# A second plain pair in the second feed-forward network, and a plain down step cut in two around the last unit

## The chip, the cores and the metric

One NeuronCore of a Trainium2 chip runs the whole block. TensorE (PE) does the matrix products, VectorE (DVE) and ScalarE (ACT) the elementwise work; SyncE (SP) issues plain DMA transfers and GpSimd (POOL) those that also convert or accumulate. The metric is the device time of one execution in microseconds.

## The reference

A decoder block on 512 tokens of width 1024, in float32. The change concerns its two gated feed-forward networks (hidden width 2816) and the first product behind the first of them.

```python
def swiglu(x, w_gate, w_up, w_down):
    return (jax.nn.silu(x @ w_gate) * (x @ w_up)) @ w_down

h = h + 0.5 * swiglu(rms_norm(h, g_ffn1[i]), w_ffn1_gate[i], w_ffn1_up[i], w_ffn1_down[i])
u = rms_norm(h, g_mix[i])
z = u @ w_in[i]
...
h = h + (g_a * y_conv + g_b * y_attn) @ w_mix_out[i]
h = h + 0.5 * swiglu(rms_norm(h, g_ffn2[i]), w_ffn2_gate[i], w_ffn2_up[i], w_ffn2_down[i])
```

## The kernel before

**Numbers.** Every float32 operand is used as a high and a low part, and a product is three matmuls (high x high, high x low, low x high). Weights get their parts in one of two ways. Either SP loads them into `wr`, ACT copies the high part (`wh`) and DVE subtracts (`wl`), in `split_one`. Or ACT writes the negated copy to `wl` and a POOL transfer adds the weights on top (`remainder`, L369 and L371); for keys in `by_dma` that are not products, POOL also loads `wh`. The gate and up weights of the second network's plain pairs are of this last kind, those of the first network's go through SP.

**Stages of a network.** `ffn` handles the 22 blocks of 128 hidden columns as 11 pairs. A pair is computed in one of two ways:

- plain: `plain` runs the gate half and then the up half; each half uses two weight slabs of 128 x 1024 and has eight steps k, each of six matmuls of 512 columns;
- as a unit, `gate_up`: seven Strassen-Winograd products B11, B21, T2, T1, T3, B22, T4 in this order, each of 24 matmuls of 256 columns, with their own weight slab. DVE makes the weights' sums (L337 to L350) and the operands' differences. `forms` makes the operands of T1 and T2 and returns `others`, which makes those of T3 and T4 (L827 to L840).

`token` works out the norm factors (a chain on DVE), `factor` spreads them to all partitions (two matmuls into a bank, an ACT copy, `R`), and `gated` multiplies a plain pair's banks by R, applies silu and multiplies gate and up (L815 to L818). The first network has two plain pairs (0 and 1), the second has one (0), and its pair 1 is a unit.

The down product runs in rounds: `down` takes two pairs as seven products of twelve 512-column matmuls, in banks `pa`, `pe`, `pd`; B11, T2, T3 and T4 build up in the same two banks `pa`, so T2 may not begin before DVE has added B11's result to the residual rows (`add`, L757). `down_plain` does pair 0 without products, in two halves of output columns (`x_` 0 and 1), each of 24 matmuls and four accumulates on DVE (L1005). `keep` queues the parts of a finished pair, `form` queues the 13 jobs that make the operands of a down round. Jobs in the list `later` are run a few at a time by `gate_up` (QUOTA) and `down_plain`, or where a product cannot begin without them.

**Order of the weights.** `slab_order` lists all weight slabs. `slab(key)` hands out the next one and, at that point of the program, issues the preparations of those behind it: loads (`load_one`), sums (`sum_one`), POOL parts (`early_one`) and splits (`split_one`), some two to seven slabs ahead. All slabs, parts, sums and the units' results share 16 buffers of 128 x 1024, so a load can wait for a buffer on its queue. PSUM has six banks for most work and two more with the tag `cv`.

Every engine runs its instructions in the order in which the program issues them (`manual_schedule`). `over(xs, ...)` transposes the finished rows into blocks and makes their parts; the last four blocks are made within the first steps of the next product: at step 2 of the first plain half of the second network (`rest`, called `soon_` inside `ffn`), and at step 2 of the first pair of `w_in` slabs.

Of the kernel before, what the change touches and what calls it, by code (L numbers as in the profile page):

```python
# [14 lines left out]
OP = mybir.AluOpType  # L15
# [3 lines left out]
P = 128  # L19
# [26 lines left out]
RAW = 4  # L46
AHEAD = 2

N_NORM = ((0, 6), (1, 3))
FINAL = ("B21", "T3", "B22", "T4")  # L50
HOLD = 4
LEAD = {"T4": 5, "B11": 3, "B21": 3}
# [12 lines left out]
A11, A12, A21, A22 = range(4)  # L65
PRODUCTS = ("B11", "B21", "T2", "T1", "T3", "B22", "T4")
MIXED = ("B11", "T1", "T2", "B22", "T3", "B21", "T4")
EARLY = {"1": 2, "2": 1}


ROUNDS = ((0, 1), (1, 2), (3, 2), (5, 2), (7, 2), (9, 2))

PLAN = (("gu", 2), ("gu", 3), ("dn", 1), ("gu", 4), ("gu", 5), ("dn", 2), ("gu", 6), ("gu", 7), ("dn", 3),
        ("gu", 8), ("gu", 9), ("dn", 4), ("gu", 10), ("dp", 0), ("dn", 5))
HELD = (3, 5, 7)
BY_ = False
N_FORM = 10
# [39 lines left out]


def ffn_order(n):
    out = [("gq", n, j, q) for j in range(EARLY[n]) for q in range(4)]  # L120
    for step in (("gu", 1),) * (EARLY[n] == 1) + PLAN:
        if step[0] == "dp":
            out += [("dp", n, step[1], x_) for x_ in range(2)]
        else:
            out += [(n, step, q) for q in PRODUCTS]
    return out
# [24 lines left out]
def block_kernel(ctx: ExitStack, tc: tile.TileContext, a, out):  # L151
# [283 lines left out]
            early_one()  # L435

    def slab(key):
        i = state["use"]
        assert order[i] == key, (order[i], key)
        state["use"] = i + 1  # L440
        more, sums = (1, 1) if key[0] == "gq" else (MORE, SUMS)
        ahead_ = AHEAD + (key[0] == "co" and key[1] >= 3)
        for j in range(i + 1, i + ahead_ + sums + 1):
            ahead("load", load_one, j + 1)
            ahead("sum", sum_one, j + 1)
            soon_(i, j)
            ahead("split", split_one, min(j, i + ahead_) + 1)
        if state["early"] < len(order) and product(order[state["early"]]) == "T4":
            soon_(i, i + LEAD["T4"])
        ahead("load", load_one, i + ahead_ + RAW + 1 + (2 if key[0] in ("pT", "pp", "pg") else 0))  # L450
        if product(order[min(i + ahead_ + RAW, len(order) - 1)]):
            ahead("load", load_one, i + ahead_ + RAW + more + 1)
        return halves.pop(i)

    def mm3(ps, wh, wl, xh, xl, start, stop, part=False):
        PE.matmul(ps, wh, xh, start=start, stop=False, skip_group_check=part)  # L456
# [317 lines left out]
    def ffn(n, xs, u, norm, out_, soon_=None, last_=None):  # L774
# [23 lines left out]
        def plain(us_, beside):  # L798

            ps = bank("pg"), bank("pu")  # L800
            for k in range(KD):
                if k in beside:
                    beside[k]()
                if k % 4 == 0:
                    h, l = us_[k // 4]()
                for g, p in ((0, ps[0]), (4, ps[1])):
                    c = slice((g + k % 4) * P, (g + k % 4 + 1) * P)
                    mm3(p, h[:, c], l[:, c], xs[k][0], xs[k][1], k == 0, k == KD - 1)
                work(1.36)
            return ps  # L810

        def gated(pgs, pus):
            tg, tu = [T("tg") for _ in pgs], [T("tu") for _ in pus]
            for t, p in zip(tg, pgs):
                job(lambda t=t, p=p: V.tensor_mul(t, p, R[0]), v=0.69)  # L815
                job(lambda t=t: A.activation(t, t, AF.Silu), 0.63)
            for t, p, g in zip(tu, pus, tg):
                job(lambda t=t, p=p, g=g: V.tensor_mul(t, p, g), v=0.69)  # L818
            early.append(tu)
# [54 lines left out]
        def factor():  # L874
            R.append(norm.on_all("cv" if n == "1" else "ps"))

        for j in range(EARLY[n]):
            done = []
            for half in range(2):
                us_ = [lambda i=i: slab(("gq", n, j, 2 * half + i)) for i in range(2)]  # L880
                fs = {}
                if n == "2":
                    fs = {k: f for (at, k), f in zip(N_NORM, (token, factor)) if at == half}
                    if half == 0:
                        fs[2] = soon_
                elif (j, half) == (0, 1):
                    others = forms()
                    fs = {k: turns.pop(0) for k in range(KD)}
                elif (j, half) == (1, 0):
                    fs = {0: token, 4: factor}  # L890
                done.append(plain(us_, fs))
                if (j, half) == (1, 0):
                    rest = jobs[:]
                    jobs.clear()
                    gated(*before)
                    while jobs:
                        next_job()
                    jobs.extend(rest)
                    before = None
                    others()  # L900
                if n == "2" and half == 0:
                    others = forms()
            before = done
        rest = jobs[:]
        jobs.clear()
        gated(*before)
        if n == "1":
            jobs.extend(rest)
            job(lambda: (keep(1, early[1], early[1]), form()))
        else:  # L910
            others()
        work(2.9)
        done = others = before = None

        def both_halves(half):
            return bass.AP(tensor=R[0].tensor, offset=R[0].offset + half.start, ap=[R[0].ap[0], [0, 2], [1, 256]])
# [68 lines left out]
                ending[:] = [lambda q=q: finish(out_, q)] if last and q in FINAL else []  # L985
                work(k_ * 1.3)

        def down_plain(r):
            at, k_ = (2 * z for z in ROUNDS[r])
            for x_ in range(2):  # L990
                wh, wl = (z.rearrange("p (m k i) -> p k m i", m=4, k=k_) for z in slab(("dp", n, r, x_)))
                for two in ((0, 1), (2, 3)):
                    while any(at + i not in hid for i in range(k_)):
                        next_job(later)
                    each = [(bank("pd"), b, slice(b * P, (b + 1) * P)) for b in two]
                    for p, b, c in each:
                        for i in range(k_):
                            PE.matmul(p, hid[at + i][0][:, c], wh[:, i], start=i == 0, stop=False)
                            PE.matmul(p, hid[at + i][1][:, c], wh[:, i], start=False, stop=False)
                    for p, b, c in each:  # L1000
                        for i in range(k_):
                            PE.matmul(p, hid[at + i][0][:, c], wl[:, i], start=False, stop=i == k_ - 1)
                    for p, b, c in each:
                        t = h[b][:, x_ * S:(x_ + 1) * S]
                        V.scalar_tensor_tensor(t, p, half_r[0][:, b:b + 1], t, op0=OP.mult, op1=OP.add)  # L1005
                    spend(0, 1.5)
                    for _ in range(min(6, len(later))):
                        next_job(later)
                    work(2 * k_ * 0.68)
            hid.clear()  # L1010

        for key in (("gu", 1),) * (EARLY[n] == 1) + PLAN:
            if key[0] == "gu":
                if key[1] == KF // 2 - 2:
                    keep(0, early[0])
                    early[0] = None
                gate_up(key[1])
                if key[1] == KF // 2 - 1:
                    xn.clear()
                    xs.clear()  # L1020
            elif key[0] == "dp":
                while waiting:
                    form()
                down_plain(key[1])
            else:
                down(key[1])
        work(999)
# [153 lines left out]
    for c in range(KD):  # L1181
        z = c, bank("pb"), bank("pa"), T("gg"), T("glu")
        if c == 0:
            ws = [slab(("win", m)) for m in (8, 0)]
            for k in range(KD):
                if k == 2:
                    over(us, V_GM, high)
                    ending.pop()()
                i = slice(k * P, (k + 1) * P)
                for p, (wh, wl) in zip(z[1:3], ws):  # L1190
                    mm3(p, wh[:, i], wl[:, i], *us[k], k == 0, k == KD - 1)
            rcols.append(unorm.by_token())
# [606 lines left out]
```

## Time and profile before

| what | us |
|---|---|
| median of 3 runs | 1285.52 (1285.18 to 1288.2) |
| profiled execution, whole | 1289.34 |
| its span | 1287.2 |
| mean granted clock of TensorE | 0.995 |
| waits of PE on DVE gx L757, two times | 4.2 |
| wait of PE on DVE bl L830, once | 4.0 |

The span runs from the first to the last instruction of the profiled execution. An engine's busy time counts its instructions alone; idle time of an engine matters only where PE ends up waiting for it. In a timeline row the first number is the start, the second the duration, and the bracket gives the idle time before it and what ended it. The waits of PE have the total, how many there were, and the longest.

### The profile page before, as it was taken

To read this page: it belongs to the slowest core of one execution; us is meant where nothing else is said; L and a number is where in the kernel's file an instruction comes from. 1 tells how busy PE (TensorE), PEld (TensorE's weight loads), DVE (VectorE), ACT (ScalarE), POOL (GpSimd) and SP (SyncE) were. 2 spreads that over 40 slices of the span, in tenths; PEclk is the share of its full clock that TensorE was granted. 3 is DMA by queue.
4 is the path that set the end of the run, shared out by engine and by line. 5 is a ranking of instruction groups with operands and counts; after the bars stand their busy time and mean duration, and the time that the engine had idled before them with its cause. 6 is when DMAs were issued, how large, how long until landed. Compare 5 with 4: busy or idle time off the path is not lost. (4 is left out here: it accounts for less than half of the span.)

```text
span 1287.2 us, 19870 instructions
## 1 busy us (share of the span) xinstructions
PE 1265.8 (98%) x7466; PEld 1122.6 (87%) x7466; DVE 1062.2 (83%) x1724; ACT 750.6 (58%) x1093; POOL 229.5 (18%) x297
## 2 busy tenths in 40 slices
PE   9999999999999999999999999999899999999997
PEld 7898999999778888889898888888898999999786
DVE  6888988988789988898888643898788988987975
ACT  6576666665633354746565544366576666565573
POOL 0011111111222233323232222132011111111000
PEclk9999999999999999999999999999899999999999
DMA  7368778778878898888897778769578778777631
GB/s 269 99 153 208 169 184 202 168 196 195 182 169 205 192 179 192 161 195 145 174 180 177 165 165 214 190 126 224 130 163 211 168 182 202 169 197 180 147 99 66
DMA packets 120983, 224.94 MB, mean 175 GB/s; under 512 B 19128, under 2 KB 63544, under 8 KB 120888
## 3 DMA queue, kind: packets, MB, share of 16 engines
q0 software_dynamic: 46288, 138.96, 52.9%
q1 hardware_dynamic: 74312, 84.46, 21.1%
q8 instruction: 59, 0.97, 0.3%
q14 instruction: 36, 0.29, 0.1%
q10 hardware_dynamic: 288, 0.26, 0.1%
HBM read 166.46 MB, written 2.13 MB: 131 GB/s over the span
## 5 line engine op out<-in xcount | busy, mean ns | idle before, releaser
L371 POOL DMA_DIRECT2D wl<-wr x101 | 86.5, 856 | 622.4 <-ACT wl L369 426.8
L1147 DVE SCALAR_TENSOR_TENSOR acc<-glu,taps,acc 128x511 f32<-128x511 f32 (+14 forms) x240 | 161.2, 733 | 0.0
L400 DVE TENSOR_TENSOR wl<-s,wh 128x1024 fp32r<-128x1024 f32 x93 | 113.3, 1219 | 39.7 <-ACT wh L399 39.5
L369 ACT ACTIVATE wl<-wh 128x1024 fp32r<-128x1024 f32 x80 | 83.6, 1051 | 66.0 <-DMA wh<-in_w_in 31.4
L369 ACT ACTIVATE wl<-wr 128x1024 fp32r<-128x1024 f32 x101 | 106.1, 1050 | 19.9 <-DVE wl L400 5.7
L732 PE MATMUL pa<-bl,wh 128*128 128x256 f32 x456 | 113.6, 286 | 4.0 <-DVE bl L830 4.0
L731 PE MATMUL pa<-bh,wh 128*128 128x256 f32 x456 | 113.2, 285 | 0.3 <-DVE p L949 0.3
L383 ACT ACTIVATE wh<-wr 128x1024 fp32r<-128x1024 f32 x101 | 105.8, 1047 | 8.4 <-PE pd L746 6.2
L399 ACT ACTIVATE wh<-s 128x1024 fp32r<-128x1024 f32 x93 | 97.4, 1050 | 21.9 <-PE pd L742 10.7
L732 PEld LDWEIGHTS pa<-bl,wh 128*128 128x128 f32 x456 | 88.6, 194 | 4.5 <-DVE bl L830 4.5
L371 POOL DMA_DIRECT2D wl<-in_w_in x56 | 49.5, 885 | 226.6 <-ACT wl L369 214.2
L731 PEld LDWEIGHTS pa<-bh,wh 128*128 128x128 f32 x456 | 88.5, 194 | 0.5 <-DVE p L949 0.5
L456 PE MATMUL pq<-xsh,wh 128*128 128x512 f32 x224 | 88.7, 396 | 0.0
L457 PE MATMUL pq<-xsl,wh 128*128 128x512 f32 x224 | 87.3, 390 | 0.0
L458 PE MATMUL pq<-xsh,wl 128*128 128x512 f32 x224 | 87.3, 390 | 0.0
L456 PE MATMUL pg<-xsh,wh 128*128 128x512 f32 x176 | 70.9, 403 | 1.1 <-DVE tg L815 0.9
L457 PE MATMUL pg<-xsl,wh 128*128 128x512 f32 x176 | 69.4, 394 | 0.7 <-DVE xsl L485 0.4
L458 PE MATMUL pg<-xsh,wl 128*128 128x512 f32 x176 | 68.7, 390 | 0.0
L734 PE MATMUL pa<-bh,wl 128*128 128x256 f32 x456 | 64.8, 285 | 0.0
L936 ACT ACTIVATE p<-pa 128x512 f32<-128x512 f32 x38 | 22.7, 598 | 69.4 <-PE pa L734 69.0
L734 PEld LDWEIGHTS pa<-bh,wl 128*128 128x128 f32 x456 | 59.6, 194 | 0.0
L741 PE MATMUL pa<-wh,bh 128*128 128x512 f32 x136 | 54.6, 402 | 4.3 <-DVE gx L757 4.2
(363 smaller groups left out, 3831.5 us busy)
## 6 DMA issues: line engine op xcount, KB each, us to landing
wl<-wr POOLq DMA_DIRECT2D x101, 512.0 KB, 5.1
wh<-in_w_in POOLq DMA_DIRECT2D x56, 512.0 KB, 7.2
wl<-in_w_in POOLq DMA_DIRECT2D x56, 512.0 KB, 6.2
wr<-in_w_ffn_down SPq DMA_DIRECT2D x44, 512.0 KB, 5.1
wr<-in_w_ffn_up SPq DMA_DIRECT2D x84, 256.0 KB, 4.5
wr<-in_w_ffn_gate SPq DMA_DIRECT2D x82, 256.0 KB, 4.7
wh<-in_w_v POOLq DMA_DIRECT2D x16, 256.0 KB, 7.3
wl<-in_w_v POOLq DMA_DIRECT2D x16, 256.0 KB, 5.3
```

The lines of the kernel that those rows point to most:

```text
L369: A.activation(l.bitcast(F32R), h, AF.Copy, scale=-1.0)
L371: G.dma_start(to, src, accum_op=OP.add)
L383: A.activation(h, r, AF.Copy)
L399: A.activation(h, r, AF.Copy)
L400: V.tensor_sub(l, r, h.bitcast(F32))
L456: PE.matmul(ps, wh, xh, start=start, stop=False, skip_group_check=part)
L457: PE.matmul(ps, wh, xl, start=False, stop=False, skip_group_check=part)
L458: PE.matmul(ps, wl, xh, start=False, stop=stop, skip_group_check=part)
L731: PE.matmul(o, h[:, c], th, start=q in ("B11", "B21", "T1") and i == 0, stop=False, skip_group_check=True)
L732: PE.matmul(o, h[:, c], tl, start=False, stop=False, skip_group_check=True)
L734: PE.matmul(o, l[:, c], th, start=False, stop=i >= len(at) - 2, skip_group_check=True)
L1147: bg.append(lambda acc=acc, g=g, w=w, s=s: V.scalar_tensor_tensor(acc[:, s:], g[:, :S - s], w, acc[:, s:], op0=OP.mult, op1=OP.add))
```

## The change

1. The second network also begins with two plain pairs: eight plain slabs are loaded and prepared instead of four, and the unit of pair 1 goes. The gate of pair 0 comes under the gate half of pair 1, `others` behind that half, as in the first network; `forms` is queued at step 3 of the first half; token moves to step 1 and factor to step 6 of the second half.
2. In the first network the gate of pair 0 is issued at step 5 of the third plain half, and no longer after it.
3. The plain down of pair 0 is cut: its first half comes before unit 10, its second half after it, ahead of the last down round. Pair 0's parts are queued one unit earlier. In the second half, the forms' jobs are issued ahead of the accumulates; in the first half, none are.
4. `slab` is split into `take` and `advance`. In the plain halves and in the first pair of `w_in` slabs, the preparations of later slabs are issued two steps after the slab is taken, and so behind `over` of the last four blocks.

```diff
-EARLY = {"1": 2, "2": 1}
+EARLY = 2
...
-        ("gu", 8), ("gu", 9), ("dn", 4), ("gu", 10), ("dp", 0), ("dn", 5))
+        ("gu", 8), ("gu", 9), ("dn", 4), ("dp", 0, 0), ("gu", 10), ("dp", 0, 1), ("dn", 5))
...
     def slab(key):
+        z = take(key)
+        advance()
+        return z
+
+    taken = []
+
+    def take(key):
         i = state["use"]
         assert order[i] == key, (order[i], key)
         state["use"] = i + 1
+        taken.append((i, key))
+        return halves.pop(i)
+
+    def advance():
+
+        while taken:
+            prepare(*taken.pop(0))
+
+    def prepare(i, key):
...
                 if k % 4 == 0:
-                    h, l = us_[k // 4]()
+                    h, l = take(us_[k // 4])
+                if k % 4 == 2:
+                    advance()
...
+        def first():
+            others.append(forms())
+
+        def gate():
+            rest = jobs[:]
+            jobs.clear()
+            gated(*done.pop(0))
+            while jobs:
+                next_job()
+            jobs.extend(rest)
+
+        done, others = [], []
+        hooks = {(0, 1): {k: turns.pop(0) for k in range(KD)}, (1, 0): {0: token, 4: factor, 5: gate}} if n == "1" else {
+            (0, 0): {2: soon_, 3: first}, (0, 1): {1: token, 6: factor}, (1, 0): {0: gate}}
+        for j in range(EARLY):
+            ps = []
             for half in range(2):
...
+                ps.append(plain([("gq", n, j, 2 * half + i) for i in range(2)], hooks.get((j, half), {})))
                 if (j, half) == (1, 0):
...
+                    others.pop()()
+            done.append(ps)
+        ps = None
+        gate()
+        job(lambda: (keep(1, early[1], early[1]), form()))
...
-        def down_plain(r):
+        def down_plain(r, x_):
...
+                for _ in range(min(6 * x_, len(later))):
+                    next_job(later)
+                for p, b, c in each:
+                    t = h[b][:, x_ * S:(x_ + 1) * S]
+                    V.scalar_tensor_tensor(t, p, half_r[0][:, b:b + 1], t, op0=OP.mult, op1=OP.add)
...
-                if key[1] == KF // 2 - 2:
+                if key[1] == KF // 2 - 3:
                     keep(0, early[0])
...
-            ws = [slab(("win", m)) for m in (8, 0)]
+            ws = [take(("win", m)) for m in (8, 0)]
             for k in range(KD):
                 if k == 2:
                     over(us, V_GM, high)
                     ending.pop()()
+                    advance()
```

More of the change, by code (lines that the diff above doesn't have):

```diff
@@ L47 @@
 AHEAD = 2
-N_NORM = ((0, 6), (1, 3))
 FINAL = ("B21", "T3", "B22", "T4")
@@ L119, in ffn_order @@
 def ffn_order(n):
-    out = [("gq", n, j, q) for j in range(EARLY[n]) for q in range(4)]
-    for step in (("gu", 1),) * (EARLY[n] == 1) + PLAN:
+    out = [("gq", n, j, q) for j in range(EARLY) for q in range(4)]
+    for step in PLAN:
         if step[0] == "dp":
-            out += [("dp", n, step[1], x_) for x_ in range(2)]
+            out += [("dp", n, *step[1:])]
         else:
@@ L452, in slab @@
             ahead("load", load_one, i + ahead_ + RAW + more + 1)
-        return halves.pop(i)
     def mm3(ps, wh, wl, xh, xl, start, stop, part=False):
@@ L875, in factor @@
             R.append(norm.on_all("cv" if n == "1" else "ps"))
-        for j in range(EARLY[n]):
-            done = []
-            for half in range(2):
[L880 to L891, printed above, removed]
-                if (j, half) == (1, 0):
[L893 to L911, printed above, removed]
+        def first():
[8 more added lines that the diff above has]
+        done, others = [], []
@@ new lines, in ffn @@
+        hooks = {(0, 1): {k: turns.pop(0) for k in range(KD)}, (1, 0): {0: token, 4: factor, 5: gate}} if n == "1" else {
+            (0, 0): {2: soon_, 3: first}, (0, 1): {1: token, 6: factor}, (1, 0): {0: gate}}
+        for j in range(EARLY):
+            ps = []
+            for half in range(2):
+                if n == "1" and (j, half) == (0, 1):
+                    first()
+                ps.append(plain([("gq", n, j, 2 * half + i) for i in range(2)], hooks.get((j, half), {})))
+                if (j, half) == (1, 0):
+                    others.pop()()
+            done.append(ps)
@@ L912, in ffn @@
+        ps = None
+        gate()
+        job(lambda: (keep(1, early[1], early[1]), form()))
         work(2.9)
-        done = others = before = None
+        done = others = None
         def both_halves(half):
@@ L986, in down @@
                 work(k_ * 1.3)
-        def down_plain(r):
+        def down_plain(r, x_):
             at, k_ = (2 * z for z in ROUNDS[r])
[L990 to L1010, printed above, removed]
@@ L1012, in ffn @@
-        for key in (("gu", 1),) * (EARLY[n] == 1) + PLAN:
+            wh, wl = (z.rearrange("p (m k i) -> p k m i", m=4, k=k_) for z in slab(("dp", n, r, x_)))
+            for two in ((0, 1), (2, 3)):
+                while any(at + i not in hid for i in range(k_)):
+                    next_job(later)
+                each = [(bank("pd"), b, slice(b * P, (b + 1) * P)) for b in two]
+                for p, b, c in each:
+                    for i in range(k_):
+                        PE.matmul(p, hid[at + i][0][:, c], wh[:, i], start=i == 0, stop=False)
+                        PE.matmul(p, hid[at + i][1][:, c], wh[:, i], start=False, stop=False)
+                for p, b, c in each:
+                    for i in range(k_):
+                        PE.matmul(p, hid[at + i][0][:, c], wl[:, i], start=False, stop=i == k_ - 1)
+                for _ in range(min(6 * x_, len(later))):
+                    next_job(later)
+                for p, b, c in each:
+                    t = h[b][:, x_ * S:(x_ + 1) * S]
+                    V.scalar_tensor_tensor(t, p, half_r[0][:, b:b + 1], t, op0=OP.mult, op1=OP.add)
+                spend(0, 1.5)
+                work(2 * k_ * 0.68)
@@ L1013, in ffn @@
+            if x_:
+                hid.clear()
+        for key in PLAN:
             if key[0] == "gu":
-                if key[1] == KF // 2 - 2:
+                if key[1] == KF // 2 - 3:
                     keep(0, early[0])
@@ L1023, in ffn @@
                     form()
-                down_plain(key[1])
+                down_plain(*key[1:])
             else:
```

## The prediction

> **What bounds the kernel now.** First the head of the page and its part on busy time, for which engine is short over the whole span.
>
> ```profile
> span 1287.2 us, 19870 instructions
> ```
>
> ```profile
> PE 1265.8 (98%) x7466; PEld 1122.6 (87%) x7466; DVE 1062.2 (83%) x1724; ACT 750.6 (58%) x1093; POOL 229.5 (18%) x297
> ```
>
> TensorE is busy 98% of the span, so only two things can count: matmul time that is added or removed, and the few places where PE stands still. The second view, the waits of PE alone, lists these (total, times, longest, in us).
>
> ```profile
> PE pa L741 <- DVE gx L757: 4.2, 2, 2.6
> PE pa L732 <- DVE bl L830: 4.0, 1, 4.0
> PE warm L503 <- DVE one L497: 1.1, 1, 1.1
> PE pg L456 <- DVE tg L815: 0.9, 1, 0.9
> PE pb L456 <- ACT xsh L476: 0.8, 1, 0.8
> PE pg L457 <- DVE xsl L485: 0.4, 2, 0.2
> PE pa L731 <- DVE p L949: 0.3, 1, 0.3
> PE pb L457 <- DVE xsl L477: 0.3, 1, 0.3
> ```
>
> Apart from the warm-up and the 0.4 at L485, all of them lie where the change works: the last down round (L741), the second network's first seven-product unit (L732, L949), the gate of the first network (L815), and the first w_in pair (L476, L477). The third view, the timeline of PE, gives from start to start what the two long ones cost, with the matmuls behind them.
>
> ```profile
> 910.99 0.28 PE L731 MATMUL pa<-bh,wh 128*128 128x256 f32 x1
> ...
> 920.72 0.41 PE L731 MATMUL pd<-xsh,wh 128*128 128x256 f32 x1
> ...
> 1017.49 1.12 PE L734 MATMUL pd<-bh,wl 128*128 128x256 f32 x8
> 1020.37 1.12 PE L734 MATMUL pa<-bh,wl 128*128 128x256 f32 x8
> ...
> 1191.02 0.39 PE L998 MATMUL pd<-wh,hidh 128*128 128x512 f32 x1
> 1193.74 0.39 PE L998 MATMUL pd<-wh,hidh 128*128 128x512 f32 x1
> 1201.00 1.07 PE L746 MATMUL pe<-wl,bh 128*128 128x512 f32 x4
> 1204.69 0.62 PE L741 MATMUL pa<-wh,bh 128*128 128x512 f32 x1 [2.63 <-DVE gx L757]
> 1208.10 1.17 PE L746 MATMUL pa<-wl,bh 128*128 128x512 f32 x4
> ```
>
> An undisturbed product of a unit takes 1020.37 - 1017.49 = 2.88 us (24 matmuls of 256 columns). Twelve matmuls of 512 columns take 1193.74 - 1191.02 = 2.72 us, 0.227 each. The product T3 that starts at 910.99 takes 9.73 until 920.72, so it loses 6.85. At 1201.00 four matmuls (0.91) are followed by a gap up to 1204.69, 2.78; the next eight need 3.41 up to 1208.10 instead of 1.81, 1.60 more. That stop thus costs 4.38, not 2.63. The view by windows has the granted clock (the column before the DMA share) for it.
>
> ```profile
> 330.00:340.00 10.00, 8.42 (x37) 6.51 (x36) 10.00 (x14) 5.97 (x10) 1.95 (x3) 1.00 0.65 153
> 1200.00:1210.00 10.00, 7.37 (x26) 5.57 (x25) 9.71 (x14) 5.96 (x10) 0.86 (x1) 0.83 0.67 165
> ```
>
> In the first network the same place lies in 330 to 340. It waited 4.2 - 2.6 = 1.6 and kept the full clock; the wait of 2.63 lost it (0.83). [...]
>
> **The change part by part.** *Second plain pair, PE.* It removes seven products, 7 x 2.88 = 20.16, and adds 2 x 8 x 6 = 96 matmuls of 512 columns, 96 x 0.227 = 21.76. Nothing hides this: **+1.6**.
>
> *Second plain pair, waits.* Why T3 waits is in DVE's timeline: the last of the operations that make the T3/T4 operands, in the second network and then in the first.
>
> ```profile
> 915.76 1.89 DVE L830 TENSOR_TENSOR bl<-t,bh 128x512 fp32r<-128x512 f32 x3
> ```
>
> ```profile
> 53.76 0.68 DVE L830 TENSOR_TENSOR bl<-t,bh 128x512 fp32r<-128x512 f32 x1
> ```
>
> In the second network they end at 917.6, inside the unit whose T3 asked for them at 910.99, since DVE makes them between that unit's own sums and splits. In the first they end at 54.4, under the up half of its second plain pair (8 x 6 x 0.227 = 10.9 us of cover), and its next unit has no wait in the list. The change copies that order, so I take the whole 6.85 as gone, and the 0.3 at L949 (DVE is then no longer behind): **-7.15**. If that cover fails, it is rival D. Token and factor move 3 steps later, and gate comes under the pair's first half; four PSUM banks of pair 0 plus R plus the first of pair 1 make six, so pair 1's second bank waits for ACT's copy of R. I take 0, since factor is issued two steps before; it costs at most that copy's delay, 1 to 2 us if a blocked weight copy stands ahead of it.
>
> *Gate of the first network.* gate goes ahead of the next slab's split and sum on DVE, 3 of 8 steps earlier (3 x 1.36 us): it covers the 0.9. **-0.9.**
>
> *Weights behind the transposed chunks.* ACT's timeline at the first w_in pair:
>
> ```profile
> 357.13 1.06 ACT L369 ACTIVATE wl<-wh 128x1024 fp32r<-128x1024 f32 x1 [2.34 <-DMA wh<-in_w_in]
> ```
>
> A weight copy that waits 2.34 for its DMA stands ahead of the copies of the transposed chunks (L476). Without it they start 2.34 + 1.06 = 3.4 us earlier, more than PE's wait of 0.8 + 0.3, which goes: **-1.1**. In the plain pairs every load, sum, split, ACT copy and POOL accumulate of the next slabs is issued two steps (2.72 us) later. The transfers have slabs of 5.44 us and a lead of three of them; what that leaves is rival C. I take 0.
>
> *Plain down in two halves.* Pair 0's low parts move one unit ahead (four operations, in a unit of 20 us that carried them before without a wait): 0. Half 0 between down round 4 and unit 10 adds no matmul; its weights are asked for earlier and those of unit 10 two products later. DVE gets 5.44 us for four accumulates, 2.63 by the rows below, and so 2.8 of slack for late loads: 0, at worst 2 us each network. What matters is the last round. DVE's timeline from the end of unit 10 (PE at 1185.56, that is 1191.02 less two groups of 2.72):
>
> ```profile
> 1189.00 1.23 DVE L341 TENSOR_TENSOR s<-s,wr 128x1024 f32<-128x1024 f32 x1 [3.83 <-DMA wr<-in_w_ffn_down]
> 1190.14 0.68 DVE L959 TENSOR_TENSOR u<-p,p 128x512 f32<-128x512 f32 x1
> 1190.74 0.68 DVE L941 TENSOR_TENSOR u<-pa,p 128x512 f32<-128x512 f32 x1
> 1191.34 1.22 DVE L345 TENSOR_TENSOR wr<-wr,wr 128x1024 f32<-128x1024 f32 x1
> 1192.47 1.40 DVE L1005 SCALAR_TENSOR_TENSOR gx<-pd,half,gx 128x512 f32<-128x512 f32 x2
> ...
> 1200.04 2.72 DVE L1005 SCALAR_TENSOR_TENSOR gx<-pd,half,gx 128x512 f32<-128x512 f32 x4
> 1202.67 1.21 DVE L400 TENSOR_TENSOR wl<-s,wh 128x1024 fp32r<-128x1024 f32 x1
> 1203.81 1.40 DVE L757 SCALAR_TENSOR_TENSOR gx<-pa,half,gx 128x512 f32<-128x512 f32 x2
> ```
>
> From 1189.00 to the first half of the add at 1203.81 (0.66) DVE works 15.5 us without a break. PE has 10.88 of plain down and two products of 2.72 to cover it, 16.3 from 1185.56, but DVE began 3.44 late, behind a load: 15.5 + 3.44 - 16.3 = 2.6, the wait seen. After the change PE's cover is only 5.44 + 2 x 2.72 = 10.88. DVE's list shrinks too: the sums L341 and L345 are issued within unit 10 (one product earlier each than before, counted from its end), and four accumulates (1202.67 - 1200.04 = 2.63) belong to half 0. Between 1192.47 and 1200.04 lie four accumulates, the sum L350 (1.14, as L341) and the forms of pair 10, so the forms are 7.57 - 2.63 - 1.14 = 3.80. Left are L959 and L941 1.20, L350 1.14, forms 3.80, four accumulates 2.63, the split L400 1.14 and the half add 0.66: 10.57. That is break-even with 10.88 less some 0.3 for the last product's result. I take a wait of 0.5 in the first network, and 1.0 in the second, where the load was late: gains 1.6 - 0.5 = **1.1** and 4.38 - 1.0 = **3.4**. Bounds: no wait at all, 6.0 gained in all; or the same late load (its sums again behind the end of unit 10, 3.4 us of extra list in the second network), nothing gained there.
>
> **Sum:** +1.6 - 7.15 - 0.9 - 1.1 - 1.1 - 3.4 = **-12.05**. The profiled execution took 1289.34 around its span of 1287.2, and lies 3.8 above the median of 1285.52; the waits are its own, and I set the sum against the median: 1285.52 - 12.05 = **1273.5**.
>
> **Rivals.** *B: the last rounds keep their waits.* For: the list is break-even, and the loads of the last round are asked for one product nearer to their first sum than in a unit without a plain half. Against: one plain slab less in the buffers. It gives back 4.5: **1278.0**.
>
> *D: the change doesn't do what it says in front:* T3/T4 forms still late in the second network, for instance as the gate's jobs hold them up. For: DVE is 83% busy. Against: the first network's rows. It gives 1273.5 + 7.15 = **1280.7**.
>
> *C: late weights in the second network's plain pairs, the slower side.* Rows: cost of the two kinds of queue, the landing of w_ffn_up's transfers from 850 to 915, and a window of the w_in stage.
>
> ```profile
> q0 software_dynamic: 46288, 138.96, 52.9%
> q1 hardware_dynamic: 74312, 84.46, 21.1%
> ```
>
> ```profile
> DMA to landing us min/median/max: 2.8/8.7/13.3
> ```
>
> ```profile
> 425.00:440.00 15.00, 15.00 (x68) 12.43 (x67) 14.90 (x24) 4.45 (x5) 3.42 (x6) 1.00 1.03 250
> ```
>
> POOL's queue takes 0.529 x 1287.2 / 138.96 = 4.9 us of the 16 engines per MB, SP's 3.2. A plain slab here is two POOL transfers of 512 KB, 4.9 of its 5.44 us; four more of them replace 2 MB on SP and 1.5 MB on POOL. Against a stall: the w_in stage runs the same load at a DMA share of 1.03 with PE never idle. For it: a low part is started 2.72 us later than before, so it has 3 x 5.44 - 2.72 = 13.6 us, less ACT's 1.05: 12.5, and the slowest landing was 13.3. With every landing at 13.3, eight slabs lose 0.8 each, 6.4: 1280. **It decides against the kernel** once landings pass 12.5 + (15.9 / 8 = 2.0) = 14.5 us: with 15 us, 8 x 2.5 = 20 is lost, **1293**. [...] No trace so far shows these slabs on POOL eight in a row.
>
> **How the numbers follow.** Forecast 0.58 (1270 to 1276), B 0.19, D 0.08, C 0.15 (0.05 below 1281.7, 0.05 up to 1289.4, 0.05 above). About 0.3%, 3.9 us, is what a measurement can tell from no change. Faster: 0.58 + 0.19 + 0.08 + 0.05 = 0.90; same 0.05; slower 0.05. The range reaches below to all waits gone and the small jitter around them too, 1285.5 - 7.15 - 0.9 - 1.1 - 6.0 + 1.6 = 1272, less 2.5 of such jitter: 1269.5; above it takes in B and D's near side, 1280.0.
>
> **What would show it.** In the waits of PE, L830 and L815 vanish and L476 with them; L757 falls under 1.5 in all. The 256-column group pa<-bh,wh loses 24 matmuls (456 to 432), and pg and pu gain 16 each on L456. The granted clock is 1.00 in the windows of both last rounds. Wrong would be: PE waiting on DMA wl or wh in the plain pairs (C), on bl L830 in unit 2 (D), or on gx L757 by 2 us or more with DVE idle before a w_ffn_down load (B).

## The result and the profile after

| | before | after |
|---|---|---|
| median of 5 runs, us | 1285.18 (1284.66 to 1288.2) | 1278.47 (1276.6 to 1280.27) |
| ratio, 95% interval | | 0.9944 (0.9927 to 0.996) |
| profiled execution, span | 1289.34, 1287.2 | 1279.57, 1277.8 |

The kernel became 6.7 us faster by the medians (5.1 to 9.4 by the interval). The forecast was 12.05 faster, 1273.5; 1278.47 lies inside its range of 1269.5 to 1280.0, 5.0 above the forecast. The head of the page and its part on busy time:

```profile
span 1277.8 us, 19737 instructions
...
PE 1261.8 (99%) x7394; PEld 1118.8 (88%) x7394; DVE 1051.6 (82%) x1713; ACT 743.3 (58%) x1084; POOL 237.7 (19%) x310
```

The waits of PE after (total, times, longest):

```profile
PE pa L745 <- DVE p L956: 3.2, 2, 1.8
...
PE pd L748 <- DVE wl L399: 1.0, 1, 1.0
PE pa L755 <- DVE gx L771: 0.8, 1, 0.8
...
PE R L623 <- DVE diag L617: 0.2, 1, 0.2
...
PE pg L470 <- DVE tg L831: 0.2, 1, 0.2
```

The wait of T3 on its operands (4.0) and those of the first w_in pair (0.8 and 0.3) are gone, the gate's fell from 0.9 to 0.2, the last round's (now L771) from 4.2 to 0.8. New are 3.2 on L956 and 1.0 on L399. The timeline of PE says where; the first network's unit 10 and last round, then the second network's unit 10:

```profile
316.73 1.12 PE L748 MATMUL pd<-xsh,wl 128*128 128x256 f32 x8
319.24 0.39 PE L745 MATMUL pa<-bh,wh 128*128 128x256 f32 x1 [1.40 <-DVE p L956]
...
332.22 1.07 PE L760 MATMUL pe<-wl,bh 128*128 128x512 f32 x4
334.10 0.47 PE L755 MATMUL pa<-wh,bh 128*128 128x512 f32 x1 [0.81 <-DVE gx L771]
...
1177.36 0.28 PE L746 MATMUL pd<-xsl,wh 128*128 128x256 f32 x1
1178.60 1.21 PE L748 MATMUL pd<-xsh,wl 128*128 128x256 f32 x8 [0.95 <-DVE wl L399]
1181.60 0.39 PE L745 MATMUL pa<-bh,wh 128*128 128x256 f32 x1 [1.79 <-DVE p L956]
...
1186.03 0.43 PE L1004 MATMUL pd<-wh,hidh 128*128 128x512 f32 x1
```

With 0.12 for a matmul of 256 columns (2.88 / 24), unit 10 of the first network loses 319.24 - 316.73 - 0.96 = 1.55. In the second network it loses 1.24 - 0.12 = 1.12 ahead of B22's low part, 3.00 - 0.96 = 2.04 ahead of T4, and T4 itself takes 4.43 instead of 2.88, another 1.55: 4.71. The last round of the first network loses 1.88 - 0.91 = 0.97, that of the second nothing. The windows show the clock (the column before the DMA share):

```profile
330.00:340.00 10.00, 9.19 (x40) 7.12 (x39) 9.90 (x14) 8.14 (x12) 1.97 (x3) 1.00 0.60 132
...
1170.00:1180.00 10.00, 8.86 (x72) 8.45 (x70) 4.51 (x7) 5.20 (x8) 0.86 (x1) 1.00 0.93 240
1180.00:1190.00 10.00, 8.40 (x42) 7.71 (x43) 9.93 (x15) 5.76 (x8) 1.72 (x2) 0.83 0.58 136
1190.00:1200.00 10.00, 10.00 (x46) 8.29 (x45) 9.90 (x15) 6.56 (x9) 0.86 (x1) 1.00 0.43 80
```

Both last rounds have the full clock, as forecast; it is now lost in unit 10. DVE is idle for more than half of 1170 to 1180 (4.51 busy), just ahead of PE's wait, and then has no break. Its timeline has the reason:

```profile
314.96 1.23 DVE L399 TENSOR_TENSOR wl<-s,wh 128x1024 fp32r<-128x1024 f32 x1 [3.88 <-DMA wl<-wr]
...
1177.32 1.23 DVE L399 TENSOR_TENSOR wl<-s,wh 128x1024 fp32r<-128x1024 f32 x1 [5.48 <-DMA wl<-wr]
...
1180.87 0.68 DVE L956 TENSOR_TENSOR p<-p,pa 128x512 f32<-128x512 f32 x1
```

The split of B22's weights (L399) waits 3.88 and 5.48 us for a transfer wl<-wr. T3's result, which must be added (L956) before T4 may use bank pa, stands behind the split in DVE's queue (three small operations and a sum lie between them). The split's own data is not late. Its output takes a buffer out of which T4's weights are still being accumulated. That transfer is in POOL's timeline, beside the loads that SP issues for the last round:

```profile
307.10 0.85 POOL L370 DMA_DIRECT2D wl<-wr  x1 [11.64 <-ACT wl L368]
...
1167.85 0.86 POOL L370 DMA_DIRECT2D wl<-wr  x1 [12.49 <-ACT wl L368]
```

```profile
1166.20 3.20 SPq L267 DMA_DIRECT2D wr<-in_w_ffn_down  x4
```

The view of line 370 for each of these two alone has them land after 7.7 and 9.3 us, at 314.8 and 1177.2; the splits begin 0.1 later. The same view for all transfers of the line, with who waited for them (us, times) and their landing times:

```profile
DVE wl L399: 9.4, 2
...
DMA to landing us min/median/max: 3.8/5.6/11.7
```

Only two of DVE's splits in the whole program wait for such a transfer, and these are the two (3.88 + 5.48 = 9.4).

### The profile page after: what moved, and what is told of

Its sections match the earlier page's. It is cut to its first block, busy times and chain, and to the rows that moved or that the text cites. A ratio compares the mean times of both kernels' runs of the same rounds, so it can differ in the third digit from the quotient of the medians.

```text
span 1277.8 us, 19737 instructions
## 1 busy us (share of the span) xinstructions
PE 1261.8 (99%) x7394; PEld 1118.8 (88%) x7394; DVE 1051.6 (82%) x1713; ACT 743.3 (58%) x1084; POOL 237.7 (19%) x310
## 4 chain that ended last, share of the span: by engine, by line
PE 88%; DVE 5%; DMA 2%; issue 2%; ACT 2%; DVEq 0%; POOLq 0%; ACTq 0%
PE pa L748 5%; PE pa L745 5%; PE pa L746 5%; PE pq L470 4%; PE pq L471 4%; PE pq L472 4%; PE pg L471 3%; PE pg L470 3%; PE pg L472 3%; PE pa L755 3%; PE pa L756 3%; PE pa L760 3%; PE pd L746 2%; PE pd L748 2%; PE pd L745 2%
## 5 line engine op out<-in xcount | busy, mean ns | idle before, releaser
L399 DVE TENSOR_TENSOR wl<-s,wh 128x1024 fp32r<-128x1024 f32 x90 | 109.9, 1221 | 41.6 <-ACT wh L398 32.2
L368 ACT ACTIVATE wl<-wh 128x1024 fp32r<-128x1024 f32 x84 | 87.9, 1051 | 72.8 <-DMA wh<-in_w_in 41.3
L745 PE MATMUL pa<-bh,wh 128*128 128x256 f32 x432 | 106.8, 285 | 3.2 <-DVE p L956 3.2
L746 PE MATMUL pa<-bl,wh 128*128 128x256 f32 x432 | 106.7, 284 | 0.0
L398 ACT ACTIVATE wh<-s 128x1024 fp32r<-128x1024 f32 x90 | 94.0, 1049 | 21.2 <-PE pd L756 9.5
L470 PE MATMUL pq<-xsh,wh 128*128 128x512 f32 x224 | 88.7, 396 | 0.0
L745 PEld LDWEIGHTS pa<-bh,wh 128*128 128x128 f32 x432 | 83.3, 193 | 3.6 <-DVE p L956 3.6
L746 PEld LDWEIGHTS pa<-bl,wh 128*128 128x128 f32 x432 | 83.5, 193 | 0.0
L470 PE MATMUL pg<-xsh,wh 128*128 128x512 f32 x192 | 76.9, 401 | 0.3 <-DVE tg L831 0.2
L471 PE MATMUL pg<-xsl,wh 128*128 128x512 f32 x192 | 75.3, 392 | 0.7 <-DVE xsl L499 0.6
L472 PE MATMUL pg<-xsh,wl 128*128 128x512 f32 x192 | 75.0, 391 | 0.0
L943 ACT ACTIVATE p<-pa 128x512 f32<-128x512 f32 x36 | 21.5, 596 | 74.4 <-PE pa L748 74.0
L771 DVE SCALAR_TENSOR_TENSOR gx<-pa,half,gx 128x512 f32<-128x512 f32 x80 | 56.3, 747 | 1.6 <-PE pa L760 1.3
```

Of the source, the lines that this page charges most:

```text
L368: A.activation(l.bitcast(F32R), h, AF.Copy, scale=-1.0)
L398: A.activation(h, r, AF.Copy)
L399: V.tensor_sub(l, r, h.bitcast(F32))
L471: PE.matmul(ps, wh, xl, start=False, stop=False, skip_group_check=part)
L472: PE.matmul(ps, wl, xh, start=False, stop=stop, skip_group_check=part)
L745: PE.matmul(o, h[:, c], th, start=q in ("B11", "B21", "T1") and i == 0, stop=False, skip_group_check=True)
```

## The experiments

Ratios are to the kernel before, with 95% intervals; 0.001 is 1.3 us.

**pair**: the second plain pair and the earlier gate alone.

```diff
-        ... ("dn", 4), ("dp", 0, 0), ("gu", 10), ("dp", 0, 1), ("dn", 5))
+        ... ("dn", 4), ("gu", 10), ("dp", 0, 0), ("dp", 0, 1), ("dn", 5))
...
-                    h, l = take(us_[k // 4])
-                if k % 4 == 2:
-                    advance()
+                    h, l = slab(us_[k // 4])
...
-            ws = [take(("win", m)) for m in (8, 0)]
+            ws = [slab(("win", m)) for m in (8, 0)]
```

> The changed kernel with the plain down in one piece behind unit 10 again and with the weights prepared at the take again; what is left of the change is the second plain pair and the earlier gate of the first network. By the forecast's terms: 1.6 more of matmuls, 7.15 and 0.9 of waits gone, so about 6.5 us less than before, and no wait on bl L830 in the second network. If instead the second plain pair's weights came late, waits of PE on DMA would show in the plain halves and the gain would be under 3 us. If the median before has less of these waits than the profiled execution had, the gain is nearer to 4.

Median 1279.41, ratio 0.9943 (0.9931 to 0.9955), that is 6.4 less than the 1285.79 of the kernel before beside it. One part of the change brings as much as the whole. That it comes to the expected 6.5 is in part luck: the gate's 0.9, counted in it, is still waited for (below).

**pair_advance**: the same with the late preparation (`take`, `advance`) left as after. Only the plain down is in one piece behind unit 10, with its parts and jobs where the kernel before has them.

> The same as pair, and the weights prepared two steps after the take: only the cut of the plain down is undone. By the forecast's terms 1.1 less than pair (the wait on xsh at the first w_in pair gone). Against the changed kernel: by the forecast the cut is worth 4.5, so this kernel is 4.5 slower than the changed one. By the reading of the trace after (waits in the last round swapped for waits of 1.4, 0.95 and 1.8 inside unit 10, 6.5 by start-to-start against 6.0) the cut is worth nothing: equal to the changed kernel within 1 us.

Median 1277.5, ratio 0.9934 (0.9922 to 0.9946). Its waits of PE, beside the warm-up and ones up to 0.6 at the start:

```profile
PE pa L755 <- DVE gx L771: 2.8, 2, 2.0
...
PE pd L1008 <- DMA wl<-wr: 0.9, 1, 0.9
```

No wait in unit 10, but waits in both last rounds, 0.78 and 2.04. The kernel after has it the other way round, and is not faster.

**split_only**: the kernel before, with only the plain down in two halves, as the change has it.

```diff
-        ... ("dn", 4), ("gu", 10), ("dp", 0), ("dn", 5))
+        ... ("dn", 4), ("dp", 0, 0), ("gu", 10), ("dp", 0, 1), ("dn", 5))
...
-                if key[1] == KF // 2 - 2:
+                if key[1] == KF // 2 - 3:
```

> The kernel before with only the cut of the plain down (first half ahead of unit 10, parts queued one unit earlier, jobs ahead of the accumulates). By the forecast 4.5 less than before. By the reading of the trace after: within 1 us of before, with DVE's split of unit 10's fourth product (B22) waiting 3 us or more for an accumulate transfer, and PE waiting inside unit 10 on DVE.

Median 1289.92, ratio 1.0024 (1.0012 to 1.0036): 1.5 to 4.6 us slower. Among its waits of PE:

```profile
PE pa L731 <- DVE p L949: 3.9, 3, 1.8
PE pd L734 <- DVE wl L400: 1.2, 2, 0.9
```

They are the waits of unit 10 under this kernel's line numbers (L949 for L956, L400 for L399), and those of the last round (L757) are gone. B22's split waits 5.38 us for the transfer wl<-wr in the first network; in the second it begins at 1186.71, 0.1 after that transfer lands (1177.87 + 8.8). So the two halves by themselves move the wait, as expected, and cost time, which neither expectation had.

**nw17_nt59**: the kernel after with one buffer more for slabs (`NW` 17 for 16) and two small tiles fewer (`NT` 59 for 61).

> The changed kernel with 17 weight buffers instead of 16, paid for with 59 instead of 61 activation buffers. Theory of buffers: the split of B22 in unit 10 waits because the loads of the last round and the raw slab of the second plain half hold the buffers that it needs; with one more it does not wait for an accumulate transfer, PE has no wait inside unit 10, and the time is 4 to 6 us under that of the changed kernel. Theory of transfers: the loads of the last round slow the accumulate and would be waited for anyway, at the next sum (L336 or L340): the wait changes its name and the gain is under 1.5 us.

Median 1289.17, ratio 1.002 (1.001 to 1.0029). The split no longer waits, yet it is slower: ACT's preparation of the second plain half now stands still, ahead of the copy out of a product's bank (L943).

```profile
316.94 1.06 ACT L368 ACTIVATE wl<-wr 128x1024 fp32r<-128x1024 f32 x1 [4.77 <-issue]
...
318.84 0.58 ACT L943 ACTIVATE p<-pd 128x512 f32<-128x512 f32 x1
```

PE waits 8.1 us in two places for L943. What the 4.77 were spent on the row doesn't tell, but T4's accumulate, issued at 307.96 here, lands 8.9 us later, at 316.9, just before ACT begins; in the second network it lands 9.7 us after 1174.74, at 1184.4, and ACT begins at 1184.51. So ACT most likely waits for that transfer in DVE's place. The change of buffers shifts every later slab, and both expectations missed; a buffer more is no remedy as it stands.

**before_again** and **pair_advance_again**: both kernels unchanged, one more profiled execution each, to see whether the profile of before had shown exceptional waits.

> The kernel before once more, unchanged, for another profiled execution of it. Theory: the waits of its two last down rounds differ from execution to execution, and the profile that the prediction was made from had large ones (1.6 in the first network, 4.38 start to start in the second). In an execution near the median the two together cost 2 to 4 us instead of 6, and the waits of the front (T3 on the operands of line 830, 4.0; the gate, 0.9; the first w_in pair, 0.8 and 0.3) are the same. Rival: they are the kernel's own, and the two last rounds again cost 5.5 us or more; then the gain that the plain down in two halves was to bring was lost elsewhere.

> The kernel with the second plain pair and the late preparation, but the plain down left in one piece, unchanged, for another profiled execution. Theory: its last-round waits, 0.78 and 2.04 us in the first profile, vary by more than 1 us between executions, with the landing of the loads of w_ffn_down; unit 10 has no wait over 0.3 in either network in both executions, because the wait there belongs to the plain down in two halves. Rival: unit 10 waits here too, 1 us or more, and then the two halves are not its cause.

```profile
PE pa L732 <- DVE bl L830: 4.0, 1, 4.0
PE pa L741 <- DVE gx L757: 3.1, 2, 1.9
```

```profile
PE pa L755 <- DVE gx L771: 2.4, 2, 1.6
PE pd L1008 <- DMA wl<-wr: 2.3, 1, 2.3
```

In the kernel before (first fence) the front's waits of 4.0 and 0.9 come back to the tenth; the first w_in pair's 0.8 is 0.6. The last rounds, from their first matmul to the start of T4, take 17.99 and 20.18 us where 16.32 is undisturbed (no_t4_add below): 5.5 lost, and 6.5 in the first profile by the same measure. That is the rival's side, not the 2 to 4 of the theory. They vary, but they are the kernel's own. In pair_advance (second fence) the last rounds' 0.78 and 2.04 became 1.55 and 0.89, and the wait on a transfer in the plain down grew from 0.9 to 2.3; unit 10 has none again.

**loads_later**: the kernel after; in unit 10 every load is issued one slab later, and so behind B22's split.

```diff
+        RAW_ = RAW - (key[1:2] == (("gu", KF // 2 - 1),))
...
-        ahead("load", load_one, i + ahead_ + RAW + 1 + (2 if key[0] in ("pT", "pp", "pg") else 0))
+        ahead("load", load_one, i + ahead_ + RAW_ + 1 + (2 if key[0] in ("pT", "pp", "pg") else 0))
```

> The kernel after, with the loads that are issued in unit 10 one slab later, so that those of the second plain half and the last round stand behind the split of B22's weights and no longer ahead of it. Theory (the split waits for a buffer that T4's accumulate frees late, beside these loads): the waits of unit 10, 1.55 in the first network and 3.16 with 1.05 of slow clock in the second, fall under 0.5 each, and the split no longer waits 3.9 and 5.5 us. The sums of the last round wait for their loads instead, up to 2 us in each network: 1274 to 1279, ratio to before 0.991 to 0.995. Rival (the waits of unit 10 come from DVE having more work than the unit has time): they stay within 0.5 us of what they were.

Median 1277.14, ratio 0.9927 (0.9911 to 0.9942), not told apart from the kernel after. DVE's timeline in the second network, with the same split first:

```profile
1172.65 1.22 DVE L399 TENSOR_TENSOR wl<-s,wh 128x1024 fp32r<-128x1024 f32 x1 [0.27 <-ACT wh L398]
...
1177.75 1.23 DVE L336 TENSOR_TENSOR s<-wr,wr 128x1024 f32<-128x1024 f32 x1 [2.60 <-DMA wr<-in_w_ffn_down]
...
1181.63 1.22 DVE L340 TENSOR_TENSOR s<-s,wr 128x1024 f32<-128x1024 f32 x1 [1.46 <-DMA wr<-in_w_ffn_down]
```

The split's wait is gone, as the theory had it, and T4's accumulate now lands after 4.8 us in both networks, no longer after 7.7 and 9.3: the loads beside it had made it late. The loads are now late for the sums, by more than the 2 us expected (3.30 at L336 in the first network). PE loses less in unit 10 of the second network (0.5 at L957), but still 1.2 in the first network's, and waits 1.3 and 2.4 in the last rounds.

**loads_sums_later**: the sums of unit 10 one slab later as well (`sums` less one at the same place).

> The same, with the sums issued in unit 10 one slab later too, so that DVE doesn't stand in unit 10 behind a load that was issued late. Theory: unit 10 has no wait over 0.5 in either network; the list of DVE after the unit grows by one sum, 1.14 us, to 11.7 against 10.9 of cover, so that each last round waits about 1 us: 1274 to 1277, ratio to before 0.991 to 0.9935. Rival (DVE short of time in unit 10): the waits only move to the last round, by as much as they were, 1.5 and 3 us or more, and the time stays at 1278 to 1280.

Median 1287.12, ratio 1.0001 (0.999 to 1.0012); both theories missed. Four preparations of 1.04 us now stand in one row on ACT (311.23 to 315.0) ahead of the copy out of bank pa (L945) that the next product needs:

```profile
PE pa L747 <- ACT p L945: 5.6, 2, 2.8
PE pa L757 <- DVE gx L773: 4.1, 2, 2.5
```

Moving work about in this unit moves the wait to whatever engine gets the work, and can cost all that the change had won.

**no_t4_add**: the transfer itself is taken away, one of 512 KB per network.

```diff
-                remainder(l, r, row_of([r]))
+                remainder(l, r, row_of([r]), order[i][1:] != (("gu", KF // 2 - 1), "T4"))
...
-        for to, src in places(l, srcs):
+        for to, src in places(l, srcs) if add else ():
             G.dma_start(to, src, accum_op=OP.add)
```

> The kernel after, with the accumulate of T4's low part left out in unit 10 of both networks (its low part stays the negated high part, so the output changes); all else is issued as before, and B22's split then waits for no transfer. Theory (that split waits for the buffer that this accumulate reads until it lands, 3.9 and 5.5 us): the split's wait falls under 1 us, and PE's waits of unit 10, 1.55 and 3.16 with 1.05 of slow clock, fall under 0.5 each; the last rounds keep about what they had, 1.1 and 0. The time falls by 3 to 5.5, to 1273 to 1275.5, ratio to before 0.9905 to 0.9925. Rival (DVE and the loads of the last round set the end of each network, wherever the wait shows): the sums of lines 336 and 340 then wait for their loads, PE's waits in unit 10 and the last round together stay at 5 us or more of the 6.85, and the ratio stays within 0.0015 of the kernel after.

Median 1272.57 beside 1285.66 of before, ratio 0.9888 (0.9872 to 0.9905). Its longest wait of PE, beside the warm-up's, is at the kernel's start:

```profile
PE pg L471 <- DVE xsl L499: 0.5, 2, 0.2
```

Unit 10 and the last round wait for nothing, in either network. The rival, that DVE's work and the four loads set the end in any case, falls: with the same loads and the same DVE work, all of 1.55, 4.71 and 0.97 us are gone. DVE waits for no load there either. By the medians it is 5.9 us under the kernel after, and the intervals of the two ratios lie apart; that is a little more than the 3 to 5.5 expected, as the last round's 0.97 went too. The run takes away the wait for the buffer and 512 KB of traffic at once, and doesn't tell the two apart.

**no_adds** and **pa_no_adds**: the accumulates of the plain down's slabs left out too, with the plain down in two halves and in one piece. These slabs get their parts as T4's do: SP loads them, ACT copies, and POOL adds.

> The same with the accumulates of the plain down's four slabs left out too (their low parts stay the negated high parts). Three transfers fewer of 512 KB near the end of each network, 4.9 us of the 16 engines per MB. Theory: no wait over 0.5 in unit 10, the plain down or the last round of either network; 1270.5 to 1273.5, ratio 0.9885 to 0.991. Rival (DVE's work and the four loads alone set the end): 4 us or more of waits remain there, ratio 0.992 or above.

> The same three accumulates left out for each network in the kernel with the plain down in one piece. It tells what the two halves are worth once the transfers are out of the way. The prediction's working (DVE's list has 10.6 us against 10.9 of cover with two halves and 15.5 against 16.3 in one piece, so both are near break-even and the late load makes the difference): last-round waits of 1 to 2 us in each network stay here, and it is 2 to 4 us slower than the one with two halves and no accumulates. Rival (the two halves bring nothing in themselves): within 1 us of it.

Medians 1272.0 (1271.7 to 1272.87) and 1272.9 (1272.52 to 1273.66), ratios 0.9887 (0.987 to 0.9904) and 0.9893 (0.9879 to 0.9908). Neither has a wait in unit 10 or a last round. In the one in one piece the longest, beside the warm-up's, is at the kernel's start:

```profile
PE pg L470 <- DVE xsh L498: 0.6, 1, 0.6
```

So with the transfers out of the way the two halves are worth 0.9 us by the medians, and the ratios don't tell them apart; the 2 to 4 us of the prediction's working aren't there. The other accumulates that were left out brought nothing over no_t4_add.

**t4_dve**: a whole kernel again. In unit 10, T4's low part is made by DVE's split and not by the accumulate.

```diff
-        return (product(key) in BY_DMA or key[0] in POOLED + RAISED or key[:2] == ("gq", "2"))
+        return (product(key) in BY_DMA and key[1:] != (("gu", KF // 2 - 1), "T4") or key[0] in POOLED + RAISED or key[:2] == ("gq", "2"))
```

> The kernel after, whole, with the low part of T4's weights in unit 10 made by DVE's split (1.14 us more on DVE in each network) and not by the accumulate. Theory: B22's split waits for no transfer; the waits of unit 10 fall from 1.55 and 4.2 under 1 each; DVE's list grows by 1.14, so the last rounds wait 1 to 2 us each: 1275 to 1278, ratio 0.9915 to 0.994. Rival (DVE is the bound there): the waits grow by 1.14 in each network, 1280 to 1281.

Median 1276.36 (1276.2 to 1276.77), ratio 0.9919 (0.9905 to 0.9934): the fastest of the kernels that leave nothing out, 2.1 us under the kernel after by the medians, with intervals that overlap. Its waits of PE:

```profile
PE pa L755 <- DVE gx L771: 1.5, 2, 0.7
PE pa L745 <- DVE p L956: 1.2, 2, 0.6
```

The two networks are alike now: 0.6 in unit 10 and 0.7 in the last round of each, and the clock is kept (1.00 in 330 to 340 and in 1170 to 1200). Of the 5.9 us that the transfer costs, the split gives back about 3.8 in DVE's time and in what else was moved (1276.36 - 1272.57).

One measure fits all kernels: from the first matmul of T4 in down round 4 to that of T4 in the last round, PE's timeline has the same matmuls in each, 50.10 us undisturbed (no_t4_add, both networks). The two networks together lose 7.0 before (5.6 in before_again), 8.6 in split_only, 6.5 and 6.4 in the two profiles of pair_advance, 7.6 after and 4.0 in t4_dve. In pair they lose only 3.1, in its one profiled execution, which was its fastest run (1277.85); why stays open.

## Why the prediction came out as it did

Faster was right, the range held the time, and what "What would show it" listed came about (of L815, now L831, 0.2 is left); still nearly half of the gain that was forecast is missing.

- *Second plain pair: right.* From the last transposes ahead of the second network to the second product (B21) of unit 2, PE's timeline has, before and after:

```profile
871.89 1.03 PE L767 MATMUL tp<-ident,gx 128*128 128x128 f32 x8
...
929.72 0.28 PE L731 MATMUL pe<-xsh,wh 128*128 128x256 f32 x1
```

```profile
869.48 1.03 PE L781 MATMUL tp<-ident,gx 128*128 128x128 f32 x8
...
920.84 0.28 PE L745 MATMUL pe<-xsh,wh 128*128 128x256 f32 x1
```

  57.83 became 51.36: 6.47 less, where +1.6 and -6.85 gave 5.25. The rest was not in the sum: before, the low rate (granted clock 0.74 in 910 to 920, 0.92 in 920 to 930) reached into the product behind T3 (0.4 lost there), and the transposes and the first steps of the plain half took some 0.9 more than after. Groups show it done as said: pa<-bh,wh has 432 matmuls, pg and pu on L470 have 192 and 64 (176 and 48 before). Rivals C and D fall: PE waits nowhere for a transfer in the plain pairs, and T3 not at all.
- *Gate of the first network, -0.9: not gained, and not by the step I named.* In pair, where the gate stands as early as after but the preparation does not come late, the wait is still there:

```profile
PE pg L470 <- DVE tg L829: 0.9, 1, 0.9
```

  It falls to 0.2 only with the late preparation. That issues every split of a slab (L420) later: the one that ran at 29.58 before runs at 33.27 now, between the last copies ahead of the norm's chain, and the one behind the chain goes from 38.58 to 43.33, behind the spreading of the factor. So the chain, which began at 34.28 before, begins at 35.88 now, and the two matmuls that spread the factor are late. First DVE's and then PE's timeline of the kernel after:

```profile
33.27 1.23 DVE L420 TENSOR_TENSOR wl<-wr,wh 128x1024 fp32r<-128x1024 f32 x1 [1.74 <-ACT wh L419]
...
35.88 0.16 DVE L645 SCALAR_TENSOR_TENSOR m<-rows 128x4 f32<-128x4 f32 x1 [0.79 <-ACT sq L641]
```

```profile
39.13 0.39 PE L472 MATMUL pu<-xsh,wl 128*128 128x512 f32 x1
...
40.28 0.50 PE L623 MATMUL R<-diag,one_r 128*128 128x512 f32 x1 [0.23 <-DVE diag L617]
40.62 0.39 PE L470 MATMUL pg<-xsh,wh 128*128 128x512 f32 x1
```

  Three matmuls take 1.49 from start to start where 0.68 is due: 0.8 lost for 0.7 won. The first unit begins at 57.41 before and at 57.45 after. I had costed the late preparation in the plain halves at 0 and looked only at the transfers' side of it.
- *First w_in pair, -1.1: right.* Neither L490 nor L491 is among the waits. The medians of pair and pair_advance, 1.9 apart, go the same way, with intervals that overlap.
- *Plain down in two halves, -1.1 and -3.4: the step that failed.* The last rounds did as forecast or better: 1.6 and 4.38 became 0.97 and 0, so 5.0 went. What failed is the sentence "Half 0 between down round 4 and unit 10 adds no matmul; its weights are asked for earlier and those of unit 10 two products later", with its "0, at worst 2 us each network". There the loads, the accumulates and the buffers of unit 10 changed places, and unit 10 lost 1.55 + 4.71 = 6.3. I had counted DVE's operations behind unit 10 and not asked which buffer B22's split would write to, nor when that came free. Net, the term is +1.3 by these places of the profiles (+0.6 by the whole stretch, 7.0 to 7.6) instead of -4.5. The comparisons of times agree: +3.1 (1.5 to 4.6) on the kernel before, and no gain that can be told on the other.
- *The reading behind it led to the wrong remedy.* By its own figures DVE's list fits PE's cover in one piece (15.5 of 16.3), and a late load made the wait; yet the change shortens the list. With the accumulates left out, the plain down in one piece has no such wait, so there transfers made DVE late. That run has the second plain pair; the kernel before was not run so.
- *Setting the sum against the median* seems no large error. Taking T4's accumulate out gives 1285.66 - 1272.57 = 13.1, where the forecast's 12.05 with its last 1.5 of waits gone as well would be 13.55.

In rivals' words: B (4.5 given back, 1278.0) had the time almost to the microsecond, by luck, and the wrong place. It looked for the wait in the last rounds; it was one unit earlier. What C looked for in the plain pairs, a transfer that lands late, shows in unit 10: there T4's accumulate on POOL's queue took 9.3 us to land beside four loads of SP, in a window with a DMA share of 0.93, and 4.8 us where loads_later issues these loads later.

## What to carry to other kernels

When work is moved in a kernel with a shared pool of buffers, follow each buffer, not only each engine: a split can wait for a transfer that has nothing to do with its data (3.88 and 5.48 us here), only because that transfer still reads the buffer it is to write. Where a move only shifts a wait from one place to the next, look for the one transfer behind both and leave it out once; that showed in one run what the moves could not bring. And the spread of the times is a hint, no more: the kernels with waits behind landings spread over 2.3 to 3.7 us (pair, pair_advance, after), those without over 0.7 to 1.2 (no_t4_add, no_adds).

## What the runs showed of the hardware

In these runs the length of a wait alone doesn't tell whether TensorE's clock falls. Waits of 2.63 (before), 1.86 (before_again), 2.04 (pair_advance) and 1.79 behind one of 0.95 (after) lost it, with 0.83 in the window. Longer ones kept it: 2.33 in pair_advance_again (first fence, the wait that ends at 1180.75), and 2.54 in the first network of loads_sums_later (second fence, first row). In that same execution two waits of 2.80 on one line (L747) differ: the one that ends at 315.64 kept the clock (1.00 in 310 to 320), the one that ends at 1180.64 lost it (second row).

```profile
1180.00:1190.00 10.00, 9.25 (x41) 7.67 (x42) 7.19 (x13) 5.05 (x8) 1.56 (x2) 1.00 0.71 125
```

```profile
330.00:340.00 10.00, 6.36 (x28) 4.40 (x26) 9.87 (x17) 6.02 (x8) 1.54 (x3) 1.00 0.51 107
1180.00:1190.00 10.00, 9.36 (x65) 9.36 (x66) 6.59 (x10) 3.72 (x7) 1.17 (x2) 0.83 1.06 263
```

What tells them apart stays open. In a sum the tax of the low clock on a wait of about 2 us, 1.5 to 1.8 us where it fell here (1.55 after, 1.83 in pair_advance), can only be given as a range. Where the window kept 1.00, in the first network's last round, the twelve matmuls behind a wait of 0.81 took 0.27 more than 2.72 (after, 337.09 - 334.10), and those behind one of 1.58 took 0.23 more (before, 338.00 - 335.05).
